# Hybrid conv + RWKV-7 block on one core: the token shift's single-column operations moved from VectorE to ScalarE

## The chip, the cores and the metric

One core of a Trainium2 chip. The metric is the device time of one execution in microseconds (us), less being better. The engines go by their short names: PE is the matrix engine (TensorE), DVE is VectorE, ACT is ScalarE, POOL is GpSimd, SP issues the DMAs. Each engine takes its own instructions strictly in order, and waits for the others through semaphores.

## The reference, cut to what matters

A sequence of 2048 positions with 1024 channels goes through RMSNorm, one big input projection and then two branches (a causal convolution of width 31, and an RWKV-7 recurrence) that are gated, projected and added. The change touches only the step that mixes each projected column with its predecessor in time:

```
def _token_shift(z, mu):
    prev = jnp.pad(z, ((0, 0), (1, 0), (0, 0)))[:, :-1]
    return z + mu * (prev - z)
...
r, k, v, w_low, a_low = jnp.split(_token_shift(ts, mu), RWKV_SPLITS, axis=-1)
```

So out[t] = (1 - mu) * z[t] + mu * z[t-1], with z[-1] = 0.

## The kernel before, in words

Channels lie on the 128 partitions and time lies along the free dimension. The 2048 positions are worked off in `NB` = 4 blocks of `TB` = 512. For each block the input projection makes one [128, 512] tile in PSUM per 128 output channels (`product`, L944 to L954): 8 steps over the contraction, each of 6 matmuls of 256 columns (L316), because every fp32 operand is split into a high and a low part. These matmuls fill PE. The two PSUM buffers `ps_main` (pool `pm`) alternate; a product may start only when the readers of the product two before it are done.

A block has 16 heads, worked in four groups of two pairs. A pair (`pair`, L592) takes three projected tiles, K, R and V, and each goes through `shifted` (L565). With one more call per block for the low-rank columns (`lora_split`, L1107) that makes 4 * (24 + 1) = 100 calls. What one call does:

- L567, ACT: t1 = (1 - mu) * ps, a full [128, 512] pass out of PSUM. `mu1` holds 1 - mu.
- L569, DVE: dst[:, 1:] = mu * ps[:, 0:511] + t1[:, 1:], 511 columns.
- L571, DVE: dst[:, 0:1] = mu * carry + t1[:, 0:1], one column, where `carry` holds the last column of the block before.
- L573, DVE: carry = ps[:, 511:512], one column.

Who reads dst: for K the DVE products L642 (two, one for the even and one for the odd chunks of 64 columns) and L647, ACT's square L645 and POOL's L652; for R POOL's L670 and DVE's L672; for V PE's transposes L711 and POOL's L718; for the low-rank tile ACT's L1110.

Around this, DVE also runs the depthwise convolution as 31 passes of [128, 512] (L979, L982), the state chain of the recurrence (L870, L876 and L885, eight rounds per group, each between small matmuls L868, L874 and L881), the masks of the pair matrices (L687, read from the matmuls L684), transposes and copies for the inverse of a triangular matrix (L786, L820, L831 around the matmuls L816 and L826), and the group statistics (L914 to L923 with the reciprocal square root L136 to L141).

What sets the order. PE's order is written by the kernel itself: generator threads are woken when an estimated clock of PE says that their inputs ought to be there, and their small matmuls are put between the projection's matmuls. On the other engines the order is made by the framework's scheduler when the program is built, from priorities and its own estimate of when each instruction can start. Once built, the order is fixed. The blocks fill the profile up to about 2316 us; the output projections follow.

Of the kernel before, what the change touches and what calls it, by code (L numbers as in the profile page):

```python
# [9 lines left out]
F32 = mybir.dt.float32  # L10
F32R = mybir.dt.float32r
I32 = mybir.dt.int32
AF = mybir.ActivationFunctionType
ALU = mybir.AluOpType
# [4 lines left out]
P = 128  # L19
D = 1024  # L20
KT = D // P
TB = 512
# [54 lines left out]
T_VAL, T_GATE, T_COG, T_R, T_K, T_V, T_LORA, T_ROG, T_GC, T_GR = 0, 8, 16, 24, 32, 40, 48, 49, 57, 65  # L77
# [12 lines left out]
def hybrid_block(ctx: ExitStack, tc: tile.TileContext, x, vecs, convk, w2a2, final_g, ada, w_in, w_co, w_ro, w_o, crow, out,  # L90
                 seq=2048, groups=(0, 1, 2, 3), phase2=True, dbg=None):
    nc = tc.nc
    NB = seq // TB
# [26 lines left out]
    def vc(name, j=None):  # L120
        o, w = VOFF[name]
        return v[:, o:o + w] if j is None else v[:, o + j:o + j + 1]
# [20 lines left out]
    def flat(ap):  # L143
        return ap.rearrange("p a b -> p (a b)")
# [9 lines left out]
    def behind(i):  # L154
        tc.add_manual_dep(i.ins, lastpe[0].name,
                          mybir.DependencyInfo(mybir.DependencyClass.NoSync, mybir.DependencyReason.DATA), reason="order")
# [204 lines left out]
    c1 = late.enter_context(tc.tile_pool(name="c1", bufs=1))  # L361
# [52 lines left out]
    def dcol(name, src, s1, s2):  # L414
        t_ = c1.tile([P, VOFF[src][1]], F32, name=name)
        nc.vector.tensor_scalar(out=t_, in0=vc(src), scalar1=s1, scalar2=s2, op0=ALU.mult, op1=ALU.add)
        return t_

    mu1 = dcol("mu1", "rwkv_mu", -1.0, 1.0)
# [8 lines left out]
    ck = c1.tile([P, KT, CONVW], F32, name="ck")  # L428
    tail = c1.tile([P, KT, HALO], F32, name="tail")
    nc.vector.memset(tail, 0.0)  # L430
    carry = c1.tile([P, 25], F32, name="carry")
    nc.vector.memset(carry, 0.0)
    S = []
    for g in range(4):
        s_ = c1.tile([P, 2, P], F32, name=f"S{g}")
# [3 lines left out]
    def hx(name):  # L439
        return xp.tile([P, TB], F32, name=name, tag="hx")  # L440
# [121 lines left out]
        nc.vector.tensor_scalar(out=ck, in0=ck, scalar1=0.5, scalar2=None, op0=ALU.mult)  # L562
        return h

    def shifted(ps, mi, dst):  # L565
        t1 = e2.tile([P, TB], F32, name="t1", tag="t2", bufs=T2B)
        nc.scalar.activation(t1, ps, AF.Identity, scale=mu1[:, mi:mi + 1])  # L567
        mu = vc("rwkv_mu", mi)
        nc.vector.scalar_tensor_tensor(out=dst[:, 1:], in0=ps[:, 0:TB - 1], scalar=mu, in1=t1[:, 1:],  # L569
                                       op0=ALU.mult, op1=ALU.add)  # L570
        nc.vector.scalar_tensor_tensor(out=dst[:, 0:1], in0=carry[:, mi:mi + 1], scalar=mu, in1=t1[:, 0:1],  # L571
                                       op0=ALU.mult, op1=ALU.add)
        nc.vector.tensor_copy(carry[:, mi:mi + 1], ps[:, TB - 1:TB])  # L573

    def ch3(ap):
        return ap.rearrange("p (c t) -> p c t", t=CH)
# [15 lines left out]
    def pair(b, G, q_, pr, uv, Asb, rn, res, flags):  # L592
# [39 lines left out]
        BK = l3.tile([P, NCH // 2, 4 * CH], F32, name="BK", tag="BK", bufs=BKB)  # L632

        k = e1.tile([P, TB], F32, name="k", tag="k")
        shifted(res.pop("K"), T_K + pr - T_R, k)
        flags.add(("Kd", q_))
        k4 = k.rearrange("p (c e t) -> p c e t", e=2, t=CH)
        E1x = E1[:, :, 0:CH].rearrange("p (c e) t -> p c e t", e=2)
# [2 lines left out]
        for e in range(2):  # L641
            nc.vector.scalar_tensor_tensor(out=KR[:, :, CH * (1 + e):CH * (2 + e)], in0=k4[:, :, e, :],  # L642
                                           scalar=vc("rwkv_k_k", pr), in1=E1x[:, :, e, :], op0=ALU.mult, op1=ALU.mult)
# [5 lines left out]
                                       scalar=hkk[:, pr:pr + 1], in1=E2.rearrange("p (c n) -> p c n", n=2 * CH),  # L649
                                       op0=ALU.mult, op1=ALU.mult)  # L650
# [13 lines left out]

        yield (lambda: ("R", q_) in flags, 0.0)
        r = e1.tile([P, TB], F32, name="r", tag="r")
        shifted(res.pop("R"), pr, r)
        flags.add(("Rd", q_))
        r4 = r.rearrange("p (c e t) -> p c e t", e=2, t=CH)
        nc.gpsimd.tensor_tensor(out=outer(KR), in0=r4, in1=E1i, op=ALU.mult)  # L670
# [4 lines left out]
        for c4 in range(NCH // 4):  # L675
# [10 lines left out]
            for hh in range(2):  # L686
                nc.vector.tensor_tensor(  # L687
                    out=Asb[:, hh, c4 * 4:c4 * 4 + 4, :].rearrange("p (a e) n -> p a (e n)", e=2),
                    in0=pA[hh], in1=flat(maskA).unsqueeze(1).broadcast_to([P, 2, 256]), op=ALU.mult)
# [10 lines left out]

        yield (lambda: ("V", q_) in flags, 0.0)
        vv = e1.tile([P, TB], F32, name="vv", tag=VVT)
        shifted(res.pop("V"), T_V + pr - T_R, vv)
        rh = e1.tile([P, TB], F32R, name="rh", tag=RHT)
        nc.scalar.copy(rh, rk)
        lo = e1.tile([P, TB], F32R, name="s_lo", tag="sq")
# [285 lines left out]
    def gates(b, j, which="1234"):  # L992
        jobs = []
        for w in which:
            ti, d_ = {"1": (T_ROG, ro_dram), "2": (T_COG, co_dram), "3": (T_GR, gr_dram), "4": (T_GC, gc_dram)}[w]

            def take(ps, w=w, d_=d_):
                if w in "12":
                    silu2(ps, d_[b][j])
                else:  # L1000
                    th = e2.tile([P, TB], F32, name="th", tag="t2", bufs=T2B)
                    with tc.high_priority(HP):
                        nc.scalar.activation(th, ps, AF.Tanh, scale=0.5)
                    nc.sync.dma_start(d_[b][j], th)

            jobs.append([None, product(ti + j, take, dve()), 0])
        return jobs
# [98 lines left out]

    def lora_split(b, ps):  # L1107
        lf, ll, lx = hx("lora"), hx("lora_lo"), hx("lora_x")
        shifted(ps, T_LORA - T_R, lf)
        nc.scalar.activation(lf[0:64], lf[0:64], AF.Tanh)  # L1110
        lw = e1.tile([P, TB], F32R, name="lw", tag="lw")
        la = e1.tile([P, TB], F32R, name="la", tag="la")
        lo_, hi_ = slice(0, 64), slice(64, 128)
        parts = ((lw, lo_, hi_), (la, hi_, lo_))
        for dst, sl, _ in parts:
            nc.scalar.copy(dst[sl], lf[sl])
            nc.vector.tensor_tensor(out=ll[sl], in0=lf[sl], in1=dst[sl].bitcast(F32), op=ALU.subtract)
        yield 2 * LST
        for _, sl, os_ in parts:
            behind(nc.sync.dma_start(lx[os_], ll[sl]))  # L1120
        yield LLD
        for dst, _, os_ in parts:
            behind(nc.scalar.copy(dst[os_], lx[os_]))
        blk["lora"] = (lw, la)
        done.add(("lora", b))
# [37 lines left out]
    def steer(*jobs):  # L1163
        return [j for l in jobs for j in l]
# [185 lines left out]
    for b in range(NB):  # L1350
        for g in groups:
            G = b * len(groups) + g
            flags, R = flagd.setdefault(G, set()), rdic.setdefault(G, [{}, {}])
# [19 lines left out]
            f = steer(*[conv(b, j) if w == "c" else gates(b, j, w) for w, j in todo])  # L1373
            begin = [mark(lambda b=b, g=g: start_group(b, g))]
            if g == 0:
                if b:
                    def low(ps, b=b):
                        Thread(lora_split(b, ps), 0, HPP).resume()

                    first = [None, product(T_LORA, low), 0]  # L1380
                    begin = [mark(swap, 2, lambda b=b: ("h", b) in done), [None, duo(first, f[0]), 0]] + begin
                    f = f[1:]
# [30 lines left out]
    blk["h"] = hprep0(x0, ada_steps())  # L1413
    ctx_pe.__enter__()
    Thread(lora_split(0, front.pop(T_LORA)), 0, HPP).resume()
    for b in range(NB):
        for g in groups:
# [240 lines left out]
```

## Time and profile before

| | |
|---|---|
| three timed runs | 2931.47, 2937.36, 2937.99 us, median 2937.36 us |
| the profiled execution | 2930.53 us, span of its instructions 2928.8 us |
| granted PE clock, mean | 0.980 |
| busy share of the span | PE 95%, PE weight loads 91%, POOL 44%, DVE 69%, ACT 32% |
| busy time | PE 2774.6, DVE 2016.7, POOL 1301.1, ACT 937.3 us |

The profile is one execution of the program. It gives each instruction a start and an end, the idle time of its engine before it, and the instruction (of any engine) that ended that idle time. On DVE and ACT the end of an instruction is often later than the start of the next one on the same engine, so what an instruction takes away from its engine is better read from start to start than from its duration. A row of a group gives the count, the busy time in us, the mean duration in ns and the idle time before.

### The profile page before, as it was taken

How to read it: one execution, taken by the hardware profiler on the slowest of the kernel's cores; microseconds unless marked ns; L12 is line 12 of the kernel's file. 1: busy time of each engine (PE TensorE's matmuls, PEld its weight loads, DVE VectorE, ACT ScalarE, POOL GpSimd, SP SyncE). 2: the span in 40 equal slices, each digit the busy share in tenths (PEclk: the TensorE clock that was granted, in tenths of full speed). 3: DMA queues.
4: the chain of work that ended last, by engine and by line, in shares of the span. 5: the costliest groups of instructions: out<-in, count | busy, mean ns of one | idle time of the engine just before them, and what ended most of it. 6: DMA issues, size and time to landing. Idle time of an engine off the chain costs nothing.

```text
span 2928.8 us, 65806 instructions
## 1 busy us (share of the span) xinstructions
PE 2774.6 (95%) x26432; PEld 2651.2 (91%) x26432; DVE 2016.7 (69%) x3775; ACT 937.3 (32%) x1779; POOL 1301.1 (44%) x1814
## 2 busy tenths in 40 slices
PE   6999999899999999999999989999999999998998
PEld 6888989899999998999899989998999999986988
DVE  6695877767677787678688868686859454357633
ACT  5443334333333323233233333223322322123401
POOL 2456545743545343546455746574624320065300
PEclk9999999999999999999999999999999999999999
DMA  8776866766887776867876757765656676799674
GB/s 318 273 253 223 279 240 241 248 216 210 279 272 249 240 259 198 272 208 249 270 247 215 222 180 243 276 225 190 227 178 202 204 233 232 281 347 357 232 290 159
DMA packets 368755, 712.92 MB, mean 243 GB/s; under 512 B 129921, under 2 KB 148673, under 8 KB 368450
## 3 DMA queue, kind: packets, MB, share of 16 engines
q1 hardware_dynamic: 368450, 708.71, 72.0%
q8 instruction: 208, 3.41, 0.5%
q14 instruction: 97, 0.79, 0.1%
HBM read 515.58 MB, written 191.90 MB: 242 GB/s over the span
## 4 chain that ended last, share of the span: by engine, by line
PE 53%; DVE 15%; POOL 5%; DMA 4%; issue 2%; ACT 1%; SPq 0%; DVEq 0%; POOLq 0%; ACTq 0%
PE ps_main L316 38%; DVE acc L982 5%; PE xo L874 2%; PE xo L881 1%; PE xo L868 1%; POOL itmp L764 1%; POOL TT L768 1%; PE aux L684 1%; PE pout L1580 1%; PE pout L1578 1%; PE pout L1579 1%; PE pout L1323 1%; PE pout L1325 1%; PE pout L1324 1%; DMA As<-dT 1%
## 5 line engine op out<-in xcount | busy, mean ns | idle before, releaser
L316 PE MATMUL ps_main<-h_hi,w_hi 128*128 128x256 f32 x5120 | 1069.8, 291 | 27.6 <-issue 15.1
L316 PE MATMUL ps_main<-h_hi,w_lo 128*128 128x256 f32 x5120 | 1010.3, 279 | 3.5 <-DMA w_lo<-kl_co 1.7
L316 PE MATMUL ps_main<-h_lo,w_hi 128*128 128x256 f32 x5120 | 1011.9, 279 | 0.0
L316 PEld LDWEIGHTS ps_main<-h_hi,w_hi 128*128 128x128 f32 x5120 | 784.7, 190 | 55.0 <-issue 18.3
L316 PEld LDWEIGHTS ps_main<-h_hi,w_lo 128*128 128x128 f32 x5120 | 781.9, 190 | 4.5 <-DMA w_lo<-kl_co 2.1
L316 PEld LDWEIGHTS ps_main<-h_lo,w_hi 128*128 128x128 f32 x5120 | 785.4, 190 | 0.0
L982 DVE SCALAR_TENSOR_TENSOR acc<-u,ck,acc 128x512 f32<-128x512 f32 x928 | 697.3, 751 | 18.9
L764 POOL TENSOR_TENSOR itmp<-La,TT 128x126 f32<-128x126 f32 (+22 forms) x496 | 188.8, 381 | 74.4 <-DMA La<-dA 40.7
L768 POOL TENSOR_TENSOR TT<-TT,itmp 128x126 f32<-128x126 f32 (+22 forms) x496 | 195.3, 394 | 34.9
L295 POOL TENSOR_TENSOR w_lo<-w_st,w_hi 128x1024 fp32r<-128x1024 f32 x51 | 124.0, 2432 | 176.3 <-ACT w_hi L293 165.5
L863 ACT ACTIVATE Se<-S,pe 128x128 f32<-128x128 f32 x256 | 88.8, 395 | 270.5 <-DVE S L885 268.8
L885 DVE TENSOR_TENSOR S<-xo,Se 64x128 f32<-64x128 f32 x256 | 73.5, 287 | 125.0 <-PE xo L881 122.0
L293 ACT CAST w_hi<-w_st 128x1024 fp32r<-128x1024 f32 x71 | 74.5, 1049 | 182.0 <-DMA w_st<-w_in_t 145.8
L876 DVE TENSOR_TENSOR uv<-xo,rn 64x256 f32<-64x256 f32 x128 | 53.9, 421 | 112.1 <-PE xo L874 110.5
L652 POOL TENSOR_TENSOR ta<-ta,k 128x512 f32<-128x512 f32 x32 | 45.6, 1426 | 143.7 <-ACT ta L651 131.7
L697 POOL TENSOR_TENSOR BK<-BK,pe 128x1024 f32<-128x1024 f32 x32 | 61.2, 1913 | 100.5 <-PE aux L684 87.8
L718 POOL TENSOR_TENSOR vv<-rk,vv 128x512 f32<-128x512 f32 x32 | 42.0, 1314 | 136.0 <-ACT rk L717 122.8
L567 ACT ACTIVATE t<-ps_main,mu 128x512 f32<-128x512 f32 x96 | 65.7, 685 | 107.7 <-PE ps_main L316 104.3
L684 PE MATMUL aux<-KR,BK 64*128 64x128 f32 x1024 | 84.1, 294 | 15.8 <-DVE As L687 9.8
L870 DVE TENSOR_TENSOR XO<-xo,XO 128x256 f32<-128x256 f32 x128 | 53.6, 419 | 65.3 <-PE xo L868 64.2
L687 DVE TENSOR_TENSOR As<-aux,maskA 128x512 f32<-128x512 f32 x128 | 82.9, 682 | 22.7 <-PE aux L684 22.4
L874 PE MATMUL xo<-XO,As 64*64 64x64 f32 x1024 | 87.0, 225 | 9.4 <-DVE XO L870 8.3
(322 smaller groups left out, 4867.2 us busy)
## 6 DMA issues: line engine op xcount, KB each, us to landing
w_hi<-kh_in SPq DMA_DIRECT2D x219, 512.0 KB, 5.4
w_lo<-kl_in SPq DMA_DIRECT2D x219, 512.0 KB, 4.2
w_st<-w_in_t SPq DMA_DIRECT2D x73, 512.0 KB, 4.6
kh_in<-w_hi SPq DMA_DIRECT2D x71, 512.0 KB, 2.9
kl_in<-w_lo SPq DMA_DIRECT2D x71, 512.0 KB, 4.2
w_hi<-kh_ro SPq DMA_DIRECT2D x32, 512.0 KB, 5.3
w_lo<-kl_ro SPq DMA_DIRECT2D x32, 512.0 KB, 4.8
w_hi<-kh_co SPq DMA_DIRECT2D x32, 512.0 KB, 4.8
```

The source lines that it names most:

```text
L293: nc.scalar.copy(hi, st)
L295: lo_eng.tensor_tensor(out=lo, in0=st, in1=hi.bitcast(F32), op=ALU.subtract)
L316: lastpe[0] = te(0.113 * 2 / ms).matmul(ps[:, qs], ww[:, k, :], aa[k][:, qs], start=(k == 0 and t == 0 and q == 0), stop=(k == KT - 1 and ...
L567: nc.scalar.activation(t1, ps, AF.Identity, scale=mu1[:, mi:mi + 1])
L684: te(0.166).matmul(pA[hh][:, c // 2, es], BK[hs, cc, es], KR[hs, cc, es], start=(c == 0), stop=(c == 3), skip_group_check=True)
L687: nc.vector.tensor_tensor(out=Asb[:, hh, c4 * 4:c4 * 4 + 4, :].rearrange("p (a e) n -> p a (e n)", e=2), in0=pA[hh], in1=flat(maskA).unsqu ...
L764: first = nc.gpsimd.tensor_tensor(out=tmp[:, :ni, :nt], in0=La[:, j:j + 1, j + 1:].broadcast_to([P, ni, nt]), in1=TT[:, :ni, j:j + 1].broa ...
L768: nc.gpsimd.tensor_tensor(out=TT[:, :ni, j + 1:], in0=TT[:, :ni, j + 1:], in1=tmp[:, :ni, :nt], op=ALU.add)
L863: nc.scalar.mul(Se[:, q, :], Sg[:, q, :], R[q]["pe"][:, c:c + 1])
L874: te(0.155).matmul(xo[pr_, q, hs], As[q][pr_, hh, c, kcol(e)], XO[pr_, c, q, hs], start=(q == 0 and hh == 0), stop=(q == 1 and hh == 1), s ...
L885: nc.vector.tensor_tensor(out=Sg[hs, :, hs], in0=xo[hs, 2:4, hs], in1=Se[hs, :, hs], op=ALU.add)
L982: nc.vector.scalar_tensor_tensor(out=acc if i + 1 < HALO else yj, in0=u[:, i:i + TB], scalar=ck[:, j, i:i + 1], in1=acc, op0=ALU.mult, op1 ...
```

## The change

The two single-column steps of `shifted` go to ACT. The carry is now kept already multiplied by mu, in two tiles that take turns by blocks: block b reads `carry[b % 2]` and writes `carry[1 - b % 2]`. The first column becomes dst[:, 0:1] = (1 - mu) * ps[:, 0:1] + carry, one ACT pass with a per-partition scale and a per-partition bias, read from PSUM instead of from t1. The last block writes no carry. The full pass on DVE (L569) and the full pass on ACT (L567) stay. Line numbers are the same before and after.

```
-    carry = c1.tile([P, 25], F32, name="carry")
-    nc.vector.memset(carry, 0.0)
+    carry = [c1.tile([P, 25], F32, name=f"carry{i}") for i in range(2)]
+    nc.vector.memset(carry[0], 0.0)
...
-    def shifted(ps, mi, dst):
+    def shifted(b, ps, mi, dst):
         t1 = e2.tile([P, TB], F32, name="t1", tag="t2", bufs=T2B)
         nc.scalar.activation(t1, ps, AF.Identity, scale=mu1[:, mi:mi + 1])
         mu = vc("rwkv_mu", mi)
         nc.vector.scalar_tensor_tensor(out=dst[:, 1:], in0=ps[:, 0:TB - 1], scalar=mu, in1=t1[:, 1:],
                                        op0=ALU.mult, op1=ALU.add)
-        nc.vector.scalar_tensor_tensor(out=dst[:, 0:1], in0=carry[:, mi:mi + 1], scalar=mu, in1=t1[:, 0:1],
-                                       op0=ALU.mult, op1=ALU.add)
-        nc.vector.tensor_copy(carry[:, mi:mi + 1], ps[:, TB - 1:TB])
+        nc.scalar.activation(dst[:, 0:1], ps[:, 0:1], AF.Identity, scale=mu1[:, mi:mi + 1], bias=carry[b % 2][:, mi:mi + 1])
+        if b + 1 < NB:
+            nc.scalar.activation(carry[1 - b % 2][:, mi:mi + 1], ps[:, TB - 1:TB], AF.Identity, scale=mu)
...
-        shifted(res.pop("K"), T_K + pr - T_R, k)
+        shifted(b, res.pop("K"), T_K + pr - T_R, k)
```

(The calls for R, V and the low-rank tile get the same argument b.) So 200 DVE instructions go, and 100 + 75 ACT instructions come.

What the built programs show of the order follows. PE's order is the same in both up to the end of the blocks; later a few small matmuls of the final phase (L1508, L1518, L1530) stand some places earlier or later among the big ones. On DVE, ACT, POOL and SP neighbours have changed places in many spots.

ACT, a K call in the last block (at about 2105 us of the profile), before; in brackets the engine whose count the instruction waits for; `t` is t1, `sq` the square of k, `Dm` and `XO` belong to other work.

```order
L853 COPY XO<-aux 64x2x256 [waits DVE_49,PE_49]
L853 COPY XO<-aux 64x2x256
L567 ACTIVATE t_27636<-ps_main,mu_413 128x512 [waits PE_49]
L645 ACTIVATE sq<-k,v 128x512 [waits DVE_49]
L919 ACTIVATE Dm<-uv 128x512 [waits Pool_49]
L919 ACTIVATE Dm<-uv 128x512
```

The same place on ACT in the changed program:

```order
L853 COPY XO<-aux 64x2x256 [waits DVE_49,PE_49]
L853 COPY XO<-aux 64x2x256
L567 ACTIVATE t_27624<-ps_main,mu_413 128x512 [waits PE_49]
L571 ACTIVATE k<-ps_main,carry_435,mu_413 128x1 [waits DVE_49]
L645 ACTIVATE sq<-k,v 128x512 [waits Activation_49]
L919 ACTIVATE Dm<-uv 128x512 [waits Pool_49]
L919 ACTIVATE Dm<-uv 128x512
```

The new first-column pass stands behind L567 and waits for a DVE count. It does so in all 100 calls, and the count is the one that the L569 of the same call raises, although the two write different columns. The square then follows it on its own engine.

DVE, the V call at about 711 us, before; `As` is the masked pair matrix, `S` the state of the recurrence:

```order
L569 SCALAR_TENSOR_TENSOR vv<-ps_main,v,t_9148 128x511
L571 SCALAR_TENSOR_TENSOR vv<-carry,v,t_9148 128x1
L982 SCALAR_TENSOR_TENSOR acc<-u,ck,acc 128x512
L687 TENSOR_TENSOR As<-aux,maskA 128x512
L573 COPY carry<-ps_main 128x1
L687 TENSOR_TENSOR As<-aux,maskA 128x512
L885 TENSOR_TENSOR S_442<-xo,Se 64x2x64 x2
```

The same place on DVE in the changed program:

```order
L141 SCALAR_TENSOR_TENSOR grs<-rs_t,grs 128x16
L569 SCALAR_TENSOR_TENSOR vv<-ps_main,v,t_9149 128x511
L982 SCALAR_TENSOR_TENSOR acc<-u,ck,acc 128x512
L687 TENSOR_TENSOR As<-aux,maskA 128x512 x2
L885 TENSOR_TENSOR S_443<-xo,Se 64x2x64 x2
```

Here the two small instructions are gone and the rest stands as it did.

DVE, the V call at about 1276 us, before; `grs` is the group statistics' reciprocal square root:

```order
L982 SCALAR_TENSOR_TENSOR acc<-u,ck,acc 128x512
L569 SCALAR_TENSOR_TENSOR vv<-ps_main,v,t_16764 128x511
L141 SCALAR_TENSOR_TENSOR grs<-rs_t,grs 128x16
L571 SCALAR_TENSOR_TENSOR vv<-carry,v,t_16764 128x1
L687 TENSOR_TENSOR As<-aux,maskA 128x512
L982 SCALAR_TENSOR_TENSOR acc<-u,ck,acc 128x512
```

The same place on DVE in the changed program:

```order
L140 SCALAR_TENSOR_TENSOR rs_t<-rs_t,gst 128x16
L569 SCALAR_TENSOR_TENSOR vv<-ps_main,v,t_16765 128x511
L982 SCALAR_TENSOR_TENSOR acc<-u,ck,acc 128x512
L141 SCALAR_TENSOR_TENSOR grs<-rs_t,grs 128x16
L687 TENSOR_TENSOR As<-aux,maskA 128x512 x2
```

Here a convolution pass now stands between the shift and the masks L687, where it stood behind the first mask.

More of the change, by code (lines that the diff above doesn't have):

```diff
@@ L666, in pair @@
         r = e1.tile([P, TB], F32, name="r", tag="r")
-        shifted(res.pop("R"), pr, r)
+        shifted(b, res.pop("R"), pr, r)
         flags.add(("Rd", q_))
@@ L702, in pair @@
         vv = e1.tile([P, TB], F32, name="vv", tag=VVT)
-        shifted(res.pop("V"), T_V + pr - T_R, vv)
+        shifted(b, res.pop("V"), T_V + pr - T_R, vv)
         rh = e1.tile([P, TB], F32R, name="rh", tag=RHT)
@@ L1108, in lora_split @@
         lf, ll, lx = hx("lora"), hx("lora_lo"), hx("lora_x")
-        shifted(ps, T_LORA - T_R, lf)
+        shifted(b, ps, T_LORA - T_R, lf)
         nc.scalar.activation(lf[0:64], lf[0:64], AF.Tanh)
```

## The prediction, made before the changed kernel was run

> **What bounds the kernel now.** I read the page's head first, then the busy time of the stretch in which the shift runs (152 to 2316 us), then who ends PE's idle time there, then single places in the timeline.
>
> ```profile
> span 2928.8 us, 65806 instructions
> PE 2774.6 (95%) x26432; PEld 2651.2 (91%) x26432; DVE 2016.7 (69%) x3775; ACT 937.3 (32%) x1779; POOL 1301.1 (44%) x1814
> 152.00:2316.00 2164.00, 2074.04 (x21062) 1995.19 (x21061) 1623.57 (x3008) 729.85 (x1345) 1106.12 (x1623) 0.98 0.71 234
> ```
>
> The third row's columns are the stretch's length, then PE, PE weight loads, DVE, ACT and POOL busy, the clock and the DMA share. PE is idle for 2164.0 - 2074.0 = 90 us of this stretch; DVE is busy for 75% of it, ACT for 34%. So PE is the bound, and a change on DVE can only give back idle time of PE that a late DVE causes. The waits of PE in the same stretch, with total us, count and longest:
>
> ```profile
> PE aux L684 <- DVE As L687: 9.8, 9, 2.0
> PE xo L874 <- DVE XO L870: 8.3, 8, 1.6
> PE late L816 <- DVE T L786: 7.6, 5, 2.7
> ...
> PE late L826 <- DVE Qs L820: 5.9, 6, 1.6
> PE late L930 <- DVE As L831: 4.8, 3, 1.9
> PE xo L881 <- DVE uv L876: 4.4, 4, 2.2
> PE aux L711 <- DVE vv L571: 3.1, 1, 3.1
> PE late L895 <- DVE uv L901: 3.0, 3, 2.2
> PE ps_main L316 <- ACT th L1003: 2.4, 1, 2.4
> PE ps_main L316 <- ACT h_hi L485: 2.0, 1, 2.0
> PE xo L868 <- DVE S L885: 1.9, 1, 1.9
> ```
>
> The nine DVE rows make 48.8 us in 40 waits; the two ACT rows are the longest that ACT ends. So about 49 us, 1.7% of the time, is all that a faster DVE could bring here. None of the waits ends on a convolution pass or on L569: they end on short links that had to queue behind other DVE work.
>
> **What the change takes from DVE.** All of L571 and L573, over 0 to 2316 us:
>
> ```profile
> 0.00:2316.00 2316.00, 42.17 (x100) 0.98 0.72 238
> ```
>
> ```profile
> 0.00:2316.00 2316.00, 14.73 (x100) 0.98 0.72 238
> ```
>
> That is 42.17 + 14.73 = 56.9 us busy, 0.57 us per call. What an instruction holds back is read from its start to the next start. A usual case, and then a dear one:
>
> ```profile
> 178.75 0.20 DVE L571 SCALAR_TENSOR_TENSOR vv<-carry,v,t 128x1 f32<-128x1 f32 x1
> 178.88 0.74 DVE L982 SCALAR_TENSOR_TENSOR acc<-u,ck,acc 128x512 f32<-128x512 f32 x1
> 179.10 1.09 PE L711 MATMUL aux<-ident,vv 128*128 128x128 f32 x4 [3.15 <-DVE vv L571]
> ...
> 180.67 0.14 DVE L573 COPY carry<-ps_main 128x1 f32<-128x1 f32 x1
> 180.74 0.74 DVE L982 SCALAR_TENSOR_TENSOR acc<-u,ck,acc 128x512 f32<-128x512 f32 x1
> ```
>
> ```profile
> 710.81 0.74 DVE L569 SCALAR_TENSOR_TENSOR vv<-ps_main,v,t 128x511 f32<-128x511 f32 x1
> 710.97 1.91 POOL L923 TENSOR_TENSOR uv<-uv,grs 128x1024 f32<-128x1024 f32 x1 [1.64 <-DVE grs L141]
> 711.47 1.42 DVE L571 SCALAR_TENSOR_TENSOR vv<-carry,v,t 128x1 f32<-128x1 f32 x1
> ...
> 712.81 0.74 DVE L982 SCALAR_TENSOR_TENSOR acc<-u,ck,acc 128x512 f32<-128x512 f32 x1
> 713.47 0.68 DVE L687 TENSOR_TENSOR As<-aux,maskA 128x512 f32<-128x512 f32 x1
> 714.07 0.14 DVE L573 COPY carry<-ps_main 128x1 f32<-128x1 f32 x1
> ...
> 714.20 1.16 PE L684 MATMUL aux<-KR,BK 64*128 64x128 f32 x14 [1.47 <-DVE As L687]
> ```
>
> Usual: 178.88 - 178.75 = 0.13 us for L571 and 180.74 - 180.67 = 0.07 us for L573, 0.20 us a call. Dear: one column took 1.42 us, and it ended at 712.89, when POOL's L923 ended (710.97 + 1.91 = 712.88). Its three operands all lie in SBUF, and it waited for POOL; the pass L982 after it, begun beside no POOL work, took its 0.74. PE's wait of 1.47 us at 714.20 contains that 1.34 us (712.81 - 711.47) and 0.06 us of L573. This is the sort of wait that the change shortens.
>
> The Trainium skill ("Perfetto Trace Analysis", section "Optimizing Scalar/DVE Operations") says that a profiled latency is about twice the time the engine is held, because the write's acknowledgement overlaps the next instruction. By it DVE would get back 28 us of the 56.9; the trace agrees for usual calls (0.13 of 0.20) and not for those held by POOL.
>
> How much of it reaches PE: I went back in the timeline from each of PE's waits over 0.3 us that DVE ended, 42 between 152 and 2316 us (the first stands above, at 179.10 us; the last is below), as far as DVE had run without a pause.
>
> ```profile
> 2312.64 0.21 DVE L571 SCALAR_TENSOR_TENSOR vv<-carry,v,t 128x1 f32<-128x1 f32 x1
> ...
> 2314.10 1.16 PE L684 MATMUL aux<-KR,BK 64*128 64x128 f32 x14 [0.90 <-DVE As L687]
> ```
>
> 30 of the 42 have an L571 or L573 in that run. Taking from each wait what stood there, at most the wait itself, gives 16 us; where several waits follow one backlog and it is counted once, 12 us. At the usual 0.20 us each, 30 waits give 6 us. I take 9, half way between 6 and 12, since the calls held by POOL are real, but PE, arriving earlier, also meets the next wait earlier. Bounds for this term: 0 and -16.
>
> **What the scheduler moved.** Comparing the DVE orders at those 42 waits, the releasing instruction has one more convolution pass ahead of it at 8 of them (the piece at 1276 us is one) and less ahead of it at 5. At the start-to-start time of a pass (713.47 - 712.81 = 0.66 us) that is +5 and -3 to -5 us: I take 0, with bounds of -5 and +5.
>
> **What the change adds to ACT.** The nearest rows are one-column passes with a per-partition scale and bias (L1160) and with a bias alone (L1159), minimum, median and maximum in ns:
>
> ```profile
> L1160 ACT ACTIVATE g_col<-mod,gb,v x8: 385/386/387, 15.0 to 45.9; 128x1 f32<-128x1 f32 x8
> ```
>
> ```profile
> L1159 ACT ACTIVATE shift_col<-mod,v x8: 278/294/296, 13.5 to 44.8; 128x1 f32<-128x1 f32 x8
> ```
>
> 100 * 0.386 + 75 * 0.294 = 61 us more ACT work. On an engine that is busy for 34% this alone costs nothing; if every other cover were gone it would be 61 us, which nothing supports.
>
> **The added wait.** Each first-column pass waits on ACT for the L569 of its call, and all that is queued on ACT behind it waits too: the square L645, the casts L293 and L705, the state's scaling L863, the tanh passes that empty `ps_main`. From the end of L567 to the end of L569 the 100 calls take 0.78 to 6.50 us, 1.86 us on average; an early one in this stretch is the 178.09 us call, the last is at 2309.89 us:
>
> ```profile
> 171.97 0.69 ACT L567 ACTIVATE t<-ps_main,mu 128x512 f32<-128x512 f32 x1 [0.26 <-PE ps_main L316]
> ...
> 178.09 0.74 DVE L569 SCALAR_TENSOR_TENSOR vv<-ps_main,v,t 128x511 f32<-128x511 f32 x1
> 178.28 1.04 ACT L293 CAST w_hi<-w_st 128x1024 fp32r<-128x1024 f32 x1 [5.62 <-DMA w_st<-w_in_t]
> ```
>
> ```profile
> 2309.89 0.68 ACT L567 ACTIVATE t<-ps_main,mu 128x512 f32<-128x512 f32 x1
> ...
> 2311.98 0.74 DVE L569 SCALAR_TENSOR_TENSOR vv<-ps_main,v,t 128x511 f32<-128x511 f32 x1
> ```
>
> That is 6.17 us (172.66 to 178.83) and 2.15 us. But in these gaps ACT started little before: in the first, nothing for 5.62 us. And in K calls it already waits at this very place, at the square:
>
> ```profile
> ACT sq L645 <- DVE k L571: 32.9, 22, 6.0
> ```
>
> So I price the hold at little: no PE wait for most calls. Bounds 0 and +19 (the slower rival).
>
> **Later by a hop.** The first column is ready 0.39 us after L569 (one ACT pass) where it was ready after 0.13 to 0.20. For K, the odd-chunk product L642 does not read that column and runs meanwhile. For R, L672 has other DVE work ahead of it in 30 of 32 calls, and POOL's L670 starts some 0.2 us later. For V, PE's L711 waits 0.2 us longer where it waits at all: once before, 3.1 us. PSUM is freed by the carry pass instead of L573, at much the same time. I take +2 us in all, with bounds 0 and +5 (half of the 32 V calls at 0.2 and two R calls at 0.4, rounded up). DMAs and their queue are not touched. After 2316 us nothing of the shift runs; the few small matmuls moved there I count at 0.
>
> **The sum.** -9 + 0 + 0 + 2 = -7 us. The profiled execution took 2930.53 us (1.7 us more than its span), so such a run would take 2923.5; the median of the three runs is 6.8 us above it, and 2937.36 - 7 = 2930.4 us is my forecast. A measurement of this kernel can tell about 0.3%, 8.8 us, from no change (its runs differ by 6.5 us).
>
> **Rivals.** *Nothing comes through* (0 us, 2937.4): DVE gives time back where no wait follows, and where one follows, the scheduler has put a convolution pass there instead. For it: 8 of 42 places. Against it: the place at 711 us, where only the two small instructions went.
>
> *More comes through* (-16 us, 2921.4): each wait shrinks by all that stood ahead of it. For it: the calls held by POOL, of which the one at 711 us alone is worth 1.3 us. Against it: PE then meets the next wait.
>
> *ACT is held up* (slower): 25 calls hold ACT for over 2.5 us behind L569. If in each one the drain of `ps_main` or the state's scaling L863 comes late by a DVE pass, and PE stands 0.75 us, that is +19, and with the -7 it makes +12: 2949 us. It decides from 21 such stalls on ((8.8 + 7) / 0.75). For it: ACT is in order and the wait stands in every call. Against it: the longest wait of PE that ACT ends is 2.4 us, and the gaps were nearly empty. The Trainium skill ("ScalarE: Activation LUTs", section "Rules for kernel authors") would have additions and multiplications on VectorE and not ScalarE. By instruction the trace agrees with it (0.386 and 0.294 us against 0.13 and 0.07 from start to start); the rule does not ask which engine is waited for.
>
> **How the numbers follow.** The forecast's case has a chance of 0.50 (by its own bounds 2925 to 2937), nothing 0.25, more 0.17, slower 0.08. Faster by over 0.3%, so below 2928.6: all of "more" and three tenths of the forecast's case, 0.17 + 0.15 = 0.32. Slower: 0.08. Within 0.3%: 0.60. The range reaches down to 2921.4 less half the runs' spread, 3.3, and a little of the reordering, 2917, and up to 2937.4 + 3.3 and the hop's bound, 2943; the slower rival and the far ends of the terms stay out.
>
> **What would show it.** Right: DVE busy about 57 us less, ACT about 61 more; PE's waits on L687, L820, L870 and L876 shorter by some 6 to 9 us in all, the 1.47 us before the L684 at 714 us nearly gone; one-column ACT passes of 0.39 and 0.29 us; idle time of ACT before L571 ended by L569, near 1.9 us a call, with no new rows of PE waiting for ACT. Wrong: PE rows ended by ACT (L863, L959, L1003) that grow by over 8 us, PE's DVE rows unchanged in sum, L711 waiting in many V calls, or a difference that lies after 2316 us.

## The result, and the profile after

Seven runs of the changed kernel took 2906.30 to 2919.34 us, median 2910.56; seven of the kernel before, taken with them, 2926.32 to 2944.65, median 2932.50. The ratio is 0.9923, 95% interval 0.9902 to 0.9944: 22.6 us faster, between 16 and 29. Two more measurements of the changed kernel, e5 and e17 below, gave 0.9951 and 0.9937, so some 18 us is the better figure. The time lies below the range of the prediction (2917 to 2943 us).

The head of the page after:

```profile
span 2913.9 us, 65757 instructions
...
PE 2772.4 (95%) x26432; PEld 2649.2 (91%) x26432; DVE 1994.1 (68%) x3575; ACT 977.6 (34%) x1954; POOL 1301.7 (45%) x1814
```

And the stretch of the blocks:

```profile
152.00:2316.00 2164.00, 2085.59 (x21142) 2006.74 (x21142) 1604.67 (x2827) 772.68 (x1519) 1109.56 (x1625) 0.98 0.72 235
```

The span is 14.9 us shorter and PE's busy time 2.2, so 12.7 us of it were idle time of PE, nearly all in the blocks: there PE is now busy for 2085.6 of 2164 us instead of 2074.0. DVE's busy time fell by 22.6 us (by 28 to 30 in e5 and e17), and ACT's rose by 40.

PE's waits in that stretch, after:

```profile
PE xo L874 <- DVE XO L870: 14.4, 9, 2.8
PE late L816 <- DVE T L786: 10.2, 7, 2.7
PE ps_main L316 <- ACT carry L573: 8.0, 8, 2.0
PE aux L684 <- DVE As L687: 7.1, 9, 1.4
PE late L826 <- DVE Qs L820: 4.7, 5, 1.7
PE aux L711 <- ACT vv L571: 4.0, 1, 4.0
PE late L930 <- POOL uv L923: 3.7, 2, 2.9
...
PE xo L881 <- DVE uv L876: 2.1, 3, 0.9
```

The same view of before has a row at its head that the prediction passed over, because it names no engine:

```profile
PE ps_main L316 <- issue: 15.1, 8, 4.4
```

Added up by the engine that ended them, from 152 to 2300 us, PE's waits went from 87.7 to 75.6 us: those ended by DVE from 51.8 to 44.4, by POOL from 10.4 to 7.5, "issue" from 15.2 to nothing, and those ended by ACT from 10.3 up to 23.5. Of the 7.4 us that left DVE's rows, 3.1 are the wait of L711, which only changed its name: it now stands under ACT with 4.0. The four rows that the prediction named (L687, L820, L870 and L876) changed by 0.1 us in sum.

What "issue" hid stands in the timeline of before (start, duration, engine, line):

```profile
602.46 0.75 DVE L569 SCALAR_TENSOR_TENSOR vv<-ps_main,v,t 128x511 f32<-128x511 f32 x1
603.12 0.21 DVE L571 SCALAR_TENSOR_TENSOR vv<-carry,v,t 128x1 f32<-128x1 f32 x1
603.25 0.68 DVE L486 TENSOR_TENSOR h_lo<-hf,h_hi 128x512 fp32r<-128x512 f32 x1
603.85 1.28 DVE L687 TENSOR_TENSOR As<-aux,maskA 128x512 f32<-128x512 f32 x2
605.05 0.58 DVE L885 TENSOR_TENSOR S<-xo,Se 64x128 f32<-64x128 f32 x2
605.66 0.16 DVE L573 COPY carry<-ps_main 128x1 f32<-128x1 f32 x1
...
605.92 0.55 PE L316 MATMUL ps_main<-h_hi,w_hi 128*128 128x256 f32 x1 [3.13 <-issue]
```

PE starts 0.10 us after L573 ends, with 3.13 us of waiting behind it. L573 was the last reader of the PSUM buffer that PE wants next, and it stood on DVE behind L571, a subtraction (L486), two masks and two state updates: a 0.16 us copy let go of the buffer 2.6 us after L569, the other DVE reader, had ended (603.21). All eight "issue" waits of before (15.1 us) and three that carry another engine's name (3.2 us) end like this, 0.10 us after an L573: 18.3 us at eleven places. In the changed kernel the matching waits end 0.05 us after ACT's L573 (the 8.0 us row). So of the 12.1 us that PE's waits lost, the largest part, 10.3, is this release; DVE's rows without L711 gave 4.3 and POOL's 2.9, and ACT's other rows took some 5 back, half of it at L659, which waits for the square (0.8 us before, 3.5 after).

The place at 711 us, where L571 took 1.42 us in before, is this in the timeline after:

```profile
712.99 0.74 DVE L569 SCALAR_TENSOR_TENSOR vv<-ps_main,v,t 128x511 f32<-128x511 f32 x1
...
713.14 1.91 POOL L923 TENSOR_TENSOR uv<-uv,grs 128x1024 f32<-128x1024 f32 x1 [0.85 <-DVE grs L141]
...
713.65 0.74 DVE L982 SCALAR_TENSOR_TENSOR acc<-u,ck,acc 128x512 f32<-128x512 f32 x1
...
714.30 1.28 DVE L687 TENSOR_TENSOR As<-aux,maskA 128x512 f32<-128x512 f32 x2
...
715.04 1.16 PE L684 MATMUL aux<-KR,BK 64*128 64x128 f32 x14 [0.62 <-DVE As L687]
```

L982 follows L569 at once beside the same POOL instruction, and PE's wait is 0.62 us where it was 1.47.

### The profile page after: what moved, and what is told of

Same layout as the page of the kernel before. It is cut to its first block, busy times and chain, and to the rows that moved or that the text cites. A ratio compares the mean times of both kernels' runs of the same rounds, so it can differ in the third digit from the quotient of the medians.

```text
span 2913.9 us, 65757 instructions
## 1 busy us (share of the span) xinstructions
PE 2772.4 (95%) x26432; PEld 2649.2 (91%) x26432; DVE 1994.1 (68%) x3575; ACT 977.6 (34%) x1954; POOL 1301.7 (45%) x1814
## 4 chain that ended last, share of the span: by engine, by line
PE 54%; DVE 15%; POOL 6%; DMA 5%; issue 2%; ACT 1%; SPq 1%; DVEq 0%; POOLq 0%; ACTq 0%
PE ps_main L316 38%; DVE acc L982 5%; PE xo L874 2%; PE xo L881 1%; POOL TT L768 1%; PE aux L684 1%; PE xo L868 1%; POOL itmp L764 1%; PE pout L1580 1%; PE pout L1578 1%; PE pout L1579 1%; PE pout L1323 1%; DMA As<-dT 1%; PE pout L1325 1%; DMA w_st<-w_in_t 1%
## 5 line engine op out<-in xcount | busy, mean ns | idle before, releaser
L316 PE MATMUL ps_main<-h_hi,w_hi 128*128 128x256 f32 x5120 | 1071.3, 291 | 16.6 <-ACT carry L573 8.0
L316 PE MATMUL ps_main<-h_hi,w_lo 128*128 128x256 f32 x5120 | 1011.3, 279 | 2.9 <-POOL w_lo L295 2.3
L316 PE MATMUL ps_main<-h_lo,w_hi 128*128 128x256 f32 x5120 | 1012.4, 279 | 0.0
L316 PEld LDWEIGHTS ps_main<-h_hi,w_hi 128*128 128x128 f32 x5120 | 785.8, 191 | 44.3 <-ACT carry L573 9.8
L316 PEld LDWEIGHTS ps_main<-h_lo,w_hi 128*128 128x128 f32 x5120 | 786.8, 190 | 0.0
L316 PEld LDWEIGHTS ps_main<-h_hi,w_lo 128*128 128x128 f32 x5120 | 782.8, 190 | 3.9 <-POOL w_lo L295 2.9
L982 DVE SCALAR_TENSOR_TENSOR acc<-u,ck,acc 128x512 f32<-128x512 f32 x928 | 697.9, 752 | 18.7
L876 DVE TENSOR_TENSOR uv<-xo,rn 64x256 f32<-64x256 f32 x128 | 53.8, 421 | 113.8 <-PE xo L874 112.3
L567 ACT ACTIVATE t<-ps_main,mu 128x512 f32<-128x512 f32 x96 | 65.8, 685 | 106.3 <-PE ps_main L316 103.4
L870 DVE TENSOR_TENSOR XO<-xo,XO 128x256 f32<-128x256 f32 x128 | 53.6, 418 | 67.0 <-PE xo L868 66.1
L874 PEld LDWEIGHTS xo<-XO,As 64*64 64x64 f32 x1024 | 69.4, 135 | 32.7 <-DVE XO L870 16.2
L687 DVE TENSOR_TENSOR As<-aux,maskA 128x512 f32<-128x512 f32 x128 | 82.8, 682 | 22.5 <-PE aux L684 22.4
```

Of the source, the lines that this page charges most:

```text
L316: lastpe[0] = te(0.113 * 2 / ms).matmul(ps[:, qs], ww[:, k, :], aa[k][:, qs], start=(k == 0 and t == 0 and q == 0), stop=(k == KT - 1 and ...
L687: nc.vector.tensor_tensor(out=Asb[:, hh, c4 * 4:c4 * 4 + 4, :].rearrange("p (a e) n -> p a (e n)", e=2), in0=pA[hh], in1=flat(maskA).unsqu ...
L874: te(0.155).matmul(xo[pr_, q, hs], As[q][pr_, hh, c, kcol(e)], XO[pr_, c, q, hs], start=(q == 0 and hh == 0), stop=(q == 1 and hh == 1), s ...
L982: nc.vector.scalar_tensor_tensor(out=acc if i + 1 < HALO else yj, in0=u[:, i:i + TB], scalar=ck[:, j, i:i + 1], in1=acc, op0=ALU.mult, op1 ...
```

## The experiments

Four theories. *Release*: `ps_main` is let go sooner. *DVE time*: 200 instructions fewer on DVE; in its plain form each costs its slot (count), in its special form the price is L571, which POOL holds up (hold). *Reorder*: the scheduler happened on a better order. *Address*: the second carry tile shifts the tiles S, KR, BK and As in SBUF, and PE runs at another pace. Every kernel was timed beside the kernel before on the same chip; each ratio is to that, with its 95% interval.

**The two halves and the release.** e1 moves the carry alone:

```
-        nc.scalar.activation(dst[:, 0:1], ps[:, 0:1], AF.Identity, scale=mu1[:, mi:mi + 1], bias=carry[b % 2][:, mi:mi + 1])
+        nc.vector.tensor_tensor(out=dst[:, 0:1], in0=carry[b % 2][:, mi:mi + 1], in1=t1[:, 0:1], op=ALU.add)
```

> The carry pass alone goes to ACT (with mu, two tiles); the first column stays on DVE as t1 + carry. Release theory (the gain is the PSUM buffer of ps_main freed sooner, because its last reader no longer stands low in DVE's queue): nearly all of the 22.6 us comes, 14 to 22 us below before, and PE's waits for ps_main at L316 that in the trace of before end 0.10 us after L573 (18 us in all at ten places) fall under 10 us. DVE-time theory (200 short instructions gone): half of them are gone, so half of it, about 11 us. Reorder theory (the scheduler happened on a better order): any value, not tied to the ps_main waits.

Measured: 0.9991 (0.9981 to 1.0001). PE's waits behind L573 fell to 4.4 us, as the release theory has it, and the time hardly moved.

e2 moves the first column alone; the carry stays on DVE, low in its order:

```
-            nc.scalar.activation(carry[1 - b % 2][:, mi:mi + 1], ps[:, TB - 1:TB], AF.Identity, scale=mu)
+            nc.vector.tensor_scalar(out=carry[1 - b % 2][:, mi:mi + 1], in0=ps[:, TB - 1:TB], scalar1=mu, scalar2=None, op0=ALU.mult)
```

> The first column alone goes to ACT; the carry stays on DVE as the last reader of ps_main, multiplied by mu there. Release theory: PE's ps_main waits at L316 behind L573 stay at 13 to 20 us and the time is 0 to 8 us below before. DVE-time theory: half of the instructions are gone, and the dearer half (L571 holds DVE for POOL's counts), so 11 to 15 us below before.

Measured: 0.9977 (0.9965 to 0.9988), 6.7 us. The row of PE's waits stays:

```profile
PE ps_main L316 <- issue: 13.8, 6, 3.8
```

e3 is before with both steps early in DVE's order:

```
+        with tc.high_priority(HP):
         nc.vector.scalar_tensor_tensor(out=dst[:, 0:1], in0=carry[:, mi:mi + 1], scalar=mu, in1=t1[:, 0:1],
                                        op0=ALU.mult, op1=ALU.add)
+        with tc.high_priority(HP):
         nc.vector.tensor_copy(carry[:, mi:mi + 1], ps[:, TB - 1:TB])
```

> The computation of before, nothing moved between engines: L571 and L573 only get the scheduler's high priority, which puts L571 ahead of L569 and L573 right or almost right behind L569 in DVE's order (2.2 places behind instead of 4.3). DVE's busy time stays near 2017 us. Release theory: the ps_main waits at L316 behind L573 fall from 18 us to under 9, and the time is 8 to 16 us below before. DVE-time theory: no DVE time is freed, so within 5 us of before.

Measured: 1.0003 (0.9992 to 1.0014). Most of the late release stayed: the "issue" row fell from 15.1 to 10.8 us, and all of PE's waits that end behind an L573 from 18.3 to 13.4. So e3 says little about the release; as the whole cause it falls with e1.

e5 is the changed kernel once more:

> The changed kernel itself once more, on the chip of this call, since e1 (carry alone, ratio 0.9991) and e2 (first column alone, 0.9977) together give 9 us of the 22.6. Both halves are needed (an interaction): ratio 0.990 to 0.994 again. The parts add and the first measurement had luck of its chip: 0.996 to 0.998.

Measured: 0.9951 (0.9939 to 0.9962), 14.3 us, between the two expectations. e1 and e2 together make 9.

e8 puts the carry's line first on ACT, ahead of L567 (that part of the edit is not shown here), and takes the first column from t1, so that L569 on DVE is the last reader of `ps_main`:

```
-        nc.scalar.activation(dst[:, 0:1], ps[:, 0:1], AF.Identity, scale=mu1[:, mi:mi + 1], bias=carry[b % 2][:, mi:mi + 1])
+        nc.scalar.activation(dst[:, 0:1], t1[:, 0:1], AF.Identity, bias=carry[b % 2][:, mi:mi + 1])
```

> The changed kernel with the carry pass ahead of the full pass on ACT, and the first column taken from t1 instead of PSUM, so that the last reader of ps_main is the full DVE pass L569, not an ACT pass behind it. What is left of the release theory: PE's waits for ps_main that ACT's L573 ends (8.0 us in the trace of after) shrink to a few us, and the time is 3 to 8 us below the changed kernel of this call. DVE-time theory: the same time as the changed kernel within 4 us.

Measured: 0.9957 (0.9944 to 0.9970), level with e5. The ACT row went and a smaller one came (`PE ps_main L316 <- DVE vv L569`, 3.2 us); once L573 is off DVE, a still earlier release buys nothing that can be seen.

**DVE instructions put back.** All of these are the changed kernel with results that nobody uses, on a tile of their own. e4 puts back two per call:

```
+        nc.vector.scalar_tensor_tensor(out=junk[:, 0:1], in0=junk[:, 1:2], scalar=mu, in1=t1[:, 0:1], op0=ALU.mult, op1=ALU.add)
+        nc.vector.tensor_copy(junk[:, 1:2], t1[:, TB - 1:TB])
```

> The changed kernel with two single-column DVE instructions put back in each call, of the same kind and place as the two removed, but on a tile of their own (their results are not used) and reading t1, not ps_main. Release theory: the gain stays, 14 to 22 us below before. DVE-time theory: the gain goes, 0 to 6 us below before. If both carry half, about 10 us below.

Measured: 1.0023 (1.0013 to 1.0033). All the gain is gone, although PSUM is released as in the changed kernel (4.2 us of PE's waits behind L573, 8.0 there). But L316 ran slower in e4, since the 8-byte tile had moved other tiles; e6 gives the tile 128 bytes:

> e4 once more, with the added tile 128 bytes wide instead of 8, so that the tiles behind it (S, KR, BK, As) keep their offsets within 64 bytes, which e4 moved by 32. DVE-time theory: the 200 instructions alone undo the gain, ratio 0.998 to 1.003 as in e4 (1.0023). Address theory (in e4 the matmuls L316 ran 281 and 280 ns instead of 279 on average, some 15 us in all, because the tiles moved): PE's busy time is back at 2770 to 2775 us, and the time is at least 8 us below e4.

Measured: 1.0011 (1.0003 to 1.0020), PE busy 2775.6 us. The gain is gone without most of the address effect too (by the ratios 3.5 us below e4, not the expected 8).

e10 puts back one copy per call, and e14 two copies (columns 0 and 1 of the tile):

```
+        nc.vector.tensor_copy(junk[:, 1:2], t1[:, TB - 1:TB])
```

> The changed kernel with one short DVE copy per call put back (100 instead of e6's 200), reading t1 and writing an unused tile of 256 bytes, which leaves the addresses as they are modulo 256 bytes. DVE-time theory: half of what e6 lost without its address part (16.5 us to the changed kernel, less about 3), so 5 to 9 us above the changed kernel, ratio to before 0.997 to 0.998. If only an instruction held by another engine costs, it stays at 0.995.

Measured: 0.9936 (0.9922 to 0.9951).

> The changed kernel with two single-column copies per call put back on DVE (one operand in SBUF each). Hold theory: none of the 200 lasts over 0.3 us, and the gain stays, ratio to before 0.992 to 0.996. Count theory: as e6, which put back a copy and a scalar_tensor_tensor, 0.999 to 1.002.

Measured: 0.9913 (0.9895 to 0.9931). 100 or 200 more one-column copies on DVE cost nothing that can be seen: the count theory falls. e13 puts back the other one alone:

```
+        nc.vector.scalar_tensor_tensor(out=junk[:, 0:1], in0=junk[:, 1:2], scalar=mu, in1=t1[:, 0:1], op0=ALU.mult, op1=ALU.add)
```

> The changed kernel with one single-column scalar_tensor_tensor per call put back on DVE (two operands in SBUF, as L571 had; result unused, tile of 256 bytes). Hold theory: about a third of these 100 instructions last until the end of a POOL instruction that is running, up to 1.6 us, 20 to 25 us in all, as L571 did in before (21.3 us above the usual 0.211 us), and this alone takes back most of the gain: ratio to before 0.998 to 1.002. Count theory (each DVE instruction costs its slot): as e10, which put one copy back, 0.992 to 0.995.

Measured: 0.9981 (0.9965 to 0.9998), 13 us behind e17 and 20 behind e14 for 100 instructions. The durations (minimum, median, maximum in ns) tell why. In e13:

```profile
L571 DVE SCALAR_TENSOR_TENSOR junk<-junk,v,t x100: 197/211/1707, 55.8 to 2309.8; 128x1 f32<-128x1 f32 x100
```

In e14:

```profile
L571 DVE COPY junk<-t x200: 130/143/155, 55.9 to 2287.8; 128x1 f32<-128x1 f32 x100
```

And in before:

```profile
L571 DVE SCALAR_TENSOR_TENSOR k<-carry,v,t x32: 208/211/1421, 94.4 to 2297.7; 128x1 f32<-128x1 f32 x32
L571 DVE SCALAR_TENSOR_TENSOR r<-carry,v,t x32: 194/211/1219, 111.9 to 2304.0; 128x1 f32<-128x1 f32 x32
L571 DVE SCALAR_TENSOR_TENSOR vv<-carry,v,t x32: 200/210/1645, 127.4 to 2312.6; 128x1 f32<-128x1 f32 x32
```

The medians lie between 143 and 211 ns, and only the two-operand form has a tail. The timeline of e13, at the place of 711 us again:

```profile
714.52 0.74 DVE L569 SCALAR_TENSOR_TENSOR vv<-ps_main,v,t 128x511 f32<-128x511 f32 x1
...
714.68 1.90 POOL L923 TENSOR_TENSOR uv<-uv,grs 128x1024 f32<-128x1024 f32 x1 [0.85 <-DVE grs L141]
...
715.18 1.42 DVE L571 SCALAR_TENSOR_TENSOR junk<-junk,v,t 128x1 f32<-128x1 f32 x1
...
716.52 0.74 DVE L982 SCALAR_TENSOR_TENSOR acc<-u,ck,acc 128x512 f32<-128x512 f32 x1
717.18 1.28 DVE L687 TENSOR_TENSOR As<-aux,maskA 128x512 f32<-128x512 f32 x2
...
717.91 0.83 PE L684 MATMUL aux<-KR,BK 64*128 64x128 f32 x10 [1.72 <-DVE As L687]
```

And of e14:

```profile
701.84 0.74 DVE L569 SCALAR_TENSOR_TENSOR vv<-ps_main,v,t 128x511 f32<-128x511 f32 x1
...
702.00 1.90 POOL L923 TENSOR_TENSOR uv<-uv,grs 128x1024 f32<-128x1024 f32 x1 [0.86 <-DVE grs L141]
...
702.50 0.20 DVE L571 COPY junk<-t 128x1 f32<-128x1 f32 x2
...
702.62 0.74 DVE L982 SCALAR_TENSOR_TENSOR acc<-u,ck,acc 128x512 f32<-128x512 f32 x1
```

One unused column, 1.42 us long, ends when POOL's L923 ends (716.58), and L687 and PE's L684 come late behind it; two copies at the same spot cost DVE 0.12 us. In before 32 of the 100 L571 lasted over 0.3 us, each of them ended within 20 ns of a POOL instruction's end, and together they make 21.2 us above 0.211 us apiece; in e13 it is 30 and 18.3 us; in e14, 65 of the 200 copies lay wholly beside POOL work and none was held. The Trainium skill ("SBUF — State Buffer", section "Who interferes with whom") has this rule: a DVE instruction with two inputs in SBUF contends with a GpSimd instruction that reads SBUF, not with one that only writes it; the shared ports are an exclusive lock, and the order of issue decides who waits. The trace agrees in both halves, the second on few cases: the only three L571 of before that ran beside a POOL instruction from end to end unheld stood beside memsets. A full-size pass shows the same: L982 takes one input from SBUF and one from PSUM (`acc`), and of its 960 in before 378 started while a POOL TENSOR_TENSOR ran; none lasted over 0.76 us. One case does not fit: in e1 an L571 ran unheld in 0.14 us, begun 0.03 us after POOL's L257, which is no memset.

**One operand instead of another engine.** e15 leaves both steps on DVE, with one tensor operand each:

```
+        nc.vector.tensor_scalar(out=dst[:, 0:1], in0=t1[:, 0:1], scalar1=carry[b % 2][:, mi:mi + 1], scalar2=None, op0=ALU.add)
+        if b + 1 < NB:
+            nc.vector.tensor_scalar(out=carry[1 - b % 2][:, mi:mi + 1], in0=ps[:, TB - 1:TB], scalar1=mu, scalar2=None, op0=ALU.mult)
```

> Nothing on ACT: both single-column steps stay on DVE, but with the two carry tiles times mu, so that the first column is one tensor_scalar of t1 with carry as the per-partition operand, and the carry one tensor_scalar of PSUM: one tensor operand each instead of two. Hold theory: no such instruction lasts over 0.3 us, most of the gain comes with nothing moved to another engine, ratio 0.993 to 0.997. Count theory: as before, 0.999 to 1.001. Release theory: as before too, since the last reader of ps_main is DVE's carry again, 0.998 to 1.000.

Measured: 0.9961 (0.9945 to 0.9976), 11.4 us with nothing moved to ACT. None is held:

```profile
L571 DVE TENSOR_SCALAR k<-t,carry x32: 191/204/207, 94.3 to 2293.7; 128x1 f32<-128x1 f32 x32
L571 DVE TENSOR_SCALAR r<-t,carry x32: 189/203/213, 113.4 to 2299.9; 128x1 f32<-128x1 f32 x32
L571 DVE TENSOR_SCALAR vv<-t,carry x32: 192/203/206, 129.5 to 2308.6; 128x1 f32<-128x1 f32 x32
```

In its order L573 also stands higher (mostly two places behind L569, against four in before and e2), and PE's waits behind it are fewer, 6.1 us in all, so that part of the gain can be the release. The row of those without a name:

```profile
PE ps_main L316 <- issue: 4.8, 3, 3.1
```

e16 has the first column like e15, the carry on ACT, and 192 unused bytes:

> Carry on ACT as in the changed kernel, first column on DVE as one tensor_scalar (one tensor operand), and e12's unused tile of 192 bytes. If holds and addresses add up: ratio to before 0.990 to 0.993, the fastest of all or level with e12 (0.9923). e1 was the same but for the two-operand first column and the tile, and gave 0.9991; if the two operands did not matter, this one gives 0.996 to 0.998.

Measured: 0.9961 (0.9949 to 0.9973). Better than e1 by 9 us, in which the unused tile has a part, so the two operands seem to matter there; short of the expected 0.990 to 0.993, and why is open.

**The addresses.** e7, e11 and e12 are the changed kernel with an unused tile of 32, 64 and 192 bytes per partition, e9 is before with one of 128, which puts the tiles behind it where the changed kernel has them:

```
     carry = [c1.tile([P, 25], F32, name=f"carry{i}") for i in range(2)]
+    junk = c1.tile([P, 8], F32, name="junk")
+    nc.vector.memset(junk, 0.0)
```

> The changed kernel with one unused tile of 32 bytes per partition and its memset, which moves S, KR, BK and As by 32 bytes and changes nothing else in the order. DVE-time theory: as the changed kernel. Address theory: PE's busy time rises by 10 to 18 us to about 2785 us, and the time is 8 to 18 us above the changed kernel of this call.

> The kernel before with one unused tile of 128 bytes per partition and its memset: S, KR, BK and As lie where the changed kernel has them, no operation of the token shift moves. Address theory: of the periods of the matmuls L316 from start to start in the blocks, the share at 116 ns or more falls from 0.274 to about 0.226, and the time by 2 to 3 us (about 13000 periods x 0.048 x 4.2 ns). DVE-time theory has nothing to say on this kernel; if the time fell by 10 us or more, the gain would be the tile's.

> The changed kernel with one unused tile of 64 bytes per partition. Address theory: the share of slow periods changes from 0.226 to something else, unknown which way, and the time by 0.5 us per 0.01 of share. Without it: as the changed kernel, ratio 0.995.

> The changed kernel with one unused tile of 192 bytes per partition. Address theory: another share of slow periods, and the time by 0.5 us per 0.01 of share; if it is well under 0.2, this version is faster than both kernels. Without it: as the changed kernel, ratio 0.995.

Measured: e7 0.9972 (0.9961 to 0.9983), PE busy 2784.9 us; e9 1.0005 (0.9993 to 1.0017); e11 0.9931 (0.9915 to 0.9947); e12 0.9923 (0.9909 to 0.9938). e9 excludes that the shifted tiles made the gain. e17 and e18 are the changed kernel and e12's on one chip:

> The changed kernel, as the other side of the next one on the same chip: ratio to before 0.992 to 0.996, as in its two measurements so far.

> e12's kernel (the changed kernel with an unused tile of 192 bytes) on the chip of the changed kernel. Address theory: the share of slow periods is 0.19 against 0.226 there, worth about 2 us, so a ratio 0.0005 to 0.001 below the changed kernel's of this call; if it is level or above, the 0.9923 of e12 was the chip's.

Measured: 0.9937 (0.9915 to 0.9958) and 0.9928 (0.9911 to 0.9945). The intervals overlap nearly whole, so e12 is no proven improvement on the changed kernel, and no version of these is.

**Both causes together.** Sorted by whether a two-operand column stands on DVE, and by how much of PE's waiting for `ps_main` ends within 0.11 us behind an L573:

| | released late: 13 to 18 us behind L573 | released sooner: 0 to 8 us |
|---|---|---|
| held by POOL | before 1, e9 1.0005, e3 1.0003 | e1 0.9991, e13 0.9981, e6 1.0011, e4 1.0023 |
| not held | e2 0.9977 | changed 0.9923, 0.9951, 0.9937; e10 0.9936, e14 0.9913, e11 0.9931, e12 0.9923, e18 0.9928; e8 0.9957, e15 0.9961, e16 0.9961, e7 0.9972 |

(PE runs slower in e4 and e7, see the last section.) Alone, the missing hold gives about 7 us and the sooner release at most 6 and in e6 nothing; the changed kernel has both and gives 14 to 22. Starting from it (0.9937), putting the hold back costs 13 us (e13) and putting the release back 12 (e2).

The sets also differ in the granted clock: the executions of e1 had 0.9786 on average and those of before beside them 0.9803, those of e14 0.9833 and 0.9800. An estimate: a straight line through the 275 executions of the experiments, with one level for each kernel, falls by 1.6 us for 0.001 of clock. Read from it at 0.980, the changed kernel (e5 and e17) gains 16 us, e1 5, e2 6, e13 4, e15 11 and e14 21, each give or take 2 to 3. The sorting stays, but e1 and e2 together then make 11 of 16 us, so the surplus of both over the sum is only just clear of the noise. Whether the clock differs by chance or with the kernel, no run shows.

*Reorder* is not excluded as a part. Every variant has an order of its own: apart from L571 and L573, of some 3000 DVE instructions up to 2316 us 125 stand elsewhere in e13 than in the changed kernel, and 132 in e14. As e14 keeps the gain and e13 loses it, another order alone need not cost it; no run has the order of before without the hold.

## Why the prediction was wrong

The sign was right, and the mechanism that it put first, a column held by POOL that delays PE, is real (e13 against e14). The size was not right, and two steps failed.

- **How much of it reaches PE: -9.** This term was mis-sized. It priced 30 waits at the usual 0.20 us, 6 us, and went half way to a count of 12. But the usual part is worth nothing that can be seen: 200 copies put back cost nothing (e14). The price lies in the dear cases, 32 held L571 with 21 us, of which the text had found one and called the rest real without adding them up; putting 30 such holds back (18.3 us) costs 13 us (e13). Its rival "more comes through", -16 us, named these calls and comes nearest in size (some 18 us), but that is partly luck: it is a rival about DVE's waits alone, and the larger part of what PE's waits lost in the profile came from the release.
- **"PSUM is freed by the carry pass instead of L573, at much the same time."** This step failed: the sum had this release at nothing. L573 stood about four places behind L569, and PE waited for it at eleven places, 18.3 us; 8.0 of them are left. Without it the gain falls by 12 us (e2), but alone, with the hold still there, it brought next to nothing (e1). The ceiling of 48.8 us was read from nine rows that name DVE; the largest row of the view, 15.1 us of "issue", was DVE's too.
- **The scheduler's moves at 0 and the hop at +2** were not refuted: PE's waits on L711 went from 3.1 to 4.0 us, and no run points to the order, though none excludes it.
- **Rival "ACT is held up".** Little sign of it. New rows of PE waiting for ACT did come, against the text; the largest, at L573, are the old "issue" waits under a new name, and the rest grew by some 5 us, L659's by 2.7. ACT's idle time before L571 that L569 ended is 144 us in 84 calls, 1.7 us each, close to the 1.9 forecast; the kernel is faster all the same.
- **Expected of the profile.** DVE's busy time fell by 23 to 30 us and not 57, because the 57 added up durations that overlap the next instruction: 0.20 us by 100 and the holds make 41. Some of the holds went to others: L139 to L141, two-operand instructions as well, lasted 45 us above their medians in before and 49 (e5) to 54 in the changed kernel. ACT's one-column passes took 0.35 and 0.25 us against 0.39 and 0.29. The rows L687, L820 and L876 fell by 6.2 us together, and L870's rose by 6.1, so the 6 to 9 us expected of the four did not come there; the wait at 714 us fell by 0.85 us and not by 1.47.
- **The starting value.** The forecast subtracted from a median of three runs, 2937.36 us. The median of before in the seven runs taken with the result, these three among them, is 2932.50, so 5 of the 20 us that the forecast missed by are that; in the experiments it is 2926.9 to 2930.3.

Open: why the two causes help so little singly (the runs fit a PE that waits for whichever of two late DVE instructions comes last, but no run shows the pairs); why e16 stays at 0.9961; and why e6 (copy and two-operand instruction) loses 9 us more than e13 (the latter alone), of which PE's pace explains about 3 by an estimate (12000 periods, 0.268 of them slow against 0.209, some 4 ns each).

## What to carry to other kernels

Look at the maximum beside the median before pricing a short instruction: a one-column DVE instruction with two operands in SBUF, started while POOL worked on tensors of its own, here lasted until POOL had ended (32 of 100), and rewriting it with one operand returned 11 us where moving it to another engine returned 14 to 22. Find the last reader of each PSUM buffer and its place in its engine's order, and look at what ended just before a wait that the profile calls "issue". Where two causes delay the same consumer, try both together as well: here the halves came to 9 us apart (11 at equal clock) and the whole to 14 to 22.

## What the runs showed of the hardware that was not expected

PE's own pace depends on where other tiles lie. From start to start, successive matmuls L316 in the blocks take either 113 to 114 ns or 117 to 119, in stretches of two to over sixty. The share of the slow ones goes with the layout. Counted in the traces from 152 to 2316 us, over neighbours in PE's order with a period of 110 to 124 ns, those of 116 ns or more are 0.259 and 0.260 in before and e3; 0.210 to 0.232 in the layout of the changed kernel (its three profiles, e1, e2, e8, e9 and e15); 0.454 and 0.455 in e7 and e4 (32 bytes more); 0.268 in e6; 0.18 to 0.19 in e11, e12 and e18. (The shares in the expectations of e9 and e18 come from another count and lie a little higher.) The groups by line, after:

```profile
L316 PE MATMUL ps_main<-h_hi,w_hi 128*128 128x256 f32 x5120 | 1071.3, 291 | 16.6 <-ACT carry L573 8.0 <-ACT th L1003 3.8 <-ACT w_hi L293 1.6
L316 PE MATMUL ps_main<-h_lo,w_hi 128*128 128x256 f32 x5120 | 1012.4, 279 | 0.0
L316 PE MATMUL ps_main<-h_hi,w_lo 128*128 128x256 f32 x5120 | 1011.3, 279 | 2.9 <-POOL w_lo L295 2.3 <-DVE w_lo L295 0.5
```

And in e7:

```profile
L316 PE MATMUL ps_main<-h_hi,w_hi 128*128 128x256 f32 x5120 | 1075.7, 292 | 15.0 <-ACT carry L573 6.0 <-ACT th L1003 3.9 <-DVE th L960 1.9
L316 PE MATMUL ps_main<-h_lo,w_hi 128*128 128x256 f32 x5120 | 1019.2, 281 | 0.0
L316 PE MATMUL ps_main<-h_hi,w_lo 128*128 128x256 f32 x5120 | 1017.9, 281 | 3.2 <-POOL w_lo L295 1.9 <-DMA w_lo<-kl_co 0.7 <-DVE w_lo L295 0.5
```

These matmuls' own operands lie at the same addresses in both programs, and PE's busy time differs by 12.5 us (2784.9 against 2772.4), or 9.6 against e5 (2775.3), which had e7's clock of 0.979. The share is the better sign: PE's busy time also moves between two executions of one kernel (2764.9 us in e12 at a clock of 0.984, 2774.4 in e18 at 0.980). e7 came out 6 us above e5, with intervals that meet; PE waited a little less in it (69 us against 73). Which of the moved tiles matters, and how, was not tried.
